# A decoder layer on one core: two queues for the first loads, x turned inside a job, another sharing of the last scaling

## The chip, the cores and the metric

The kernel runs on one core of one Trainium2 chip. The metric is the device time of one execution in microseconds (us), the median of several runs. The core's engines are called TensorE (PE, matmuls; PEld, its weight loads), VectorE (DVE), ScalarE (ACT), GpSimd (POOL) and SyncE (SP), which here only issues DMAs. ScalarE and GpSimd can issue DMAs too; each issuing engine has a queue of its own.

## The reference

One layer on 256 tokens of width 2048, in float32:

```python
h = rmsnorm(x, ln1)
dq, dk, dv, sq, sk, sv = split(h @ w_in)          # w_in: 2048 x 6144
mixed = concat([rmsnorm(diff_attention(rotary(dq), rotary(dk), dv, lam), diff_head_norm),
                rmsnorm(stick_breaking_attention(sq, sk, sv), sb_head_norm)])
x = x + mixed @ w_out                              # 2048 x 2048
h = rmsnorm(x, ln2)
x = x + square(relu(h @ w_mlp_in)) @ w_mlp_out     # 2048 x 8192, 8192 x 2048
out = rmsnorm(x, ln_f)
```

The two attentions have eight heads each; lam comes from four small vectors of 64. The sizes of the four weight matrices, some 200 MB together, set the work.

## The kernel before

The tokens are two tiles of 128 (t = 0, 1). Each weight matrix is read in chunks of 4 k-tiles (128 rows each) by 512 columns, 1 MB a chunk; a chunk makes two jobs of two k-tiles. For a job, `issue_conv` (L201) splits its weights into a high part `wh` (a cast on ScalarE, L214) and a low part `wl` (the difference, on VectorE, L217); the activations are held as such a pair too, and `products_acc` (L250) makes three matmuls per k-tile and token tile: high by high, high by low, low by high. A job is thus 12 matmuls of 512 columns (L260 to L262).

x lies with tokens on partitions. `x_pair` (L311) turns two k-tiles of it with four transposes on TensorE (L319) and scales them by ln1: ScalarE writes the high half (L149), VectorE the low half (L151). The scales, `g1T`, are made in the first `x_pair`: a small transpose of `rows1` and a copy on VectorE (L286). `keep_clock_up` (L291) issues matmuls on zeros that nothing reads.

Between a start and the rest the order of the work is set in two ways. In the start, TensorE, ScalarE and VectorE get their instructions in the order in which the program calls them: `START_ORDER` (L39) names the steps, x for `x_pair`, c for `issue_conv`, m for a job's matmuls. So the low half of the first weights stands behind the first x pair on VectorE. SP, GpSimd and all that comes after the start are ordered by a planner.

The loads are issued by `issue_dma` (L177), all from SP: for chunk 0 half of the columns of x's first tile, `rows1` (ln1), the first half of the chunk, the other half of x's columns, the second half of the chunk; for the next chunks one tile of x and the chunk. `small_loads` (L85), eight DMAs for ln2, the head norms, the rotary table and the four lambda vectors, follows chunk 3.

At the end, `second_token_tile` (L754) makes the last 512 columns of token tile 1 in two halves of 256 columns; `finish_tokens` (L790) then computes the scale `rf` of each token and scales the four blocks of 512 columns (nb = 0 to 3). Blocks 0 to 2 have been multiplied by ln_f before; block 3 is multiplied by `rf` and ln_f in one three-operand pass (L817). Block 1 is ScalarE's, the others VectorE's, in five pieces; each piece is written out by a DMA from SP, block 1's from ScalarE (L822).

Of the kernel before, what the change touches and what calls it, by code (L numbers as in the profile page):

```python
# [14 lines left out]
ALU = mybir.AluOpType  # L15
# [3 lines left out]
P = 128  # L19
S = 256  # L20
# [3 lines left out]
KT = D // P  # L24
NB = 512
CK = 4
HK = 2
# [8 lines left out]
LAM_INIT = 0.8 - 0.6 * math.exp(-0.3 * 0)  # L36
W_BUFS = 3
S_BUFS = 4
START_ORDER = "x0 c0 x1 c1 m0 x2 c2 m1 c3 x3 m2 x4 c4 m3 c5 x5 m4 x6 c6 m5 c7 x7 m6"  # L39
WARM0, WARM1 = 5, 4  # L40
AHEAD = 3


# [1 line left out]
def tile_hybrid_layer(  # L45
# [19 lines left out]


    nc = tc.nc
    nc.scalar.preload_act_table_set("natural_log_exp_and_others")

    cpool = ctx.enter_context(tc.tile_pool(name="cpool", bufs=1))  # L70
    wpool = ctx.enter_context(tc.tile_pool(name="wpool", bufs=W_BUFS))
    spool = ctx.enter_context(tc.tile_pool(name="spool", bufs=S_BUFS))
# [4 lines left out]
    x_v = x[0].rearrange("(t p) c -> p t c", p=P)  # L77
    xt = [cpool.tile([P, NT, NB], F32, tag=f"x{nb}", name=f"x{nb}") for nb in range(4)]

    rows1 = cpool.tile([KT, P], F32, name="rows1")  # L80
    rows2 = cpool.tile([KT + 2, P], F32, name="rows2")
    lamv = cpool.tile([P, 4, 64], F32, name="lamv")
    rope_t = cpool.tile([P, NT, 2, 16], F32, name="rope_t")

    def small_loads():  # L85
        nc.sync.dma_start(rows2[0:KT, :], ln2[0].rearrange("(k p) -> k p", p=P))
        nc.sync.dma_start(rows2[KT:KT + 1, :], diff_head_norm)
        nc.sync.dma_start(rows2[KT + 1:KT + 2, :], sb_head_norm)
        nc.sync.dma_start(rope_t, rope)
        for i, l in enumerate((lambda_q1, lambda_k1, lambda_q2, lambda_k2)):  # L90
            nc.sync.dma_start(lamv[:, i, :], l[0].partition_broadcast(P))


    idle = cpool.tile([P, NB], BF16, name="idle")
# [68 lines left out]
    chunks = []  # L163
# [11 lines left out]
    state = {"dma": 0, "conv": 0, "job": 0, "ahead": AHEAD}  # L175

    def issue_dma():  # L177
        c = state["dma"]
        if c < len(chunks):
            pool = mlp["w"] if "w" in mlp and c % 2 else wpool  # L180
            t = pool.tile([P, CK, NB], F32, tag="w", name=f"w{c}")
            if c == 0:
                for h in range(2):
                    cs = slice(h * S, (h + 1) * S)
                    nc.sync.dma_start(xt[0][:, :, cs], x_v[:, :, cs])
                    if h == 0:
                        nc.sync.dma_start(rows1, ln1[0].rearrange("(k p) -> k p", p=P))
                    nc.sync.dma_start(t[:, h * HK:(h + 1) * HK, :], chunks[0][:, h * HK:(h + 1) * HK, :])
            else:
                if c < len(xt):  # L190
                    nc.sync.dma_start(xt[c], x_v[:, :, c * NB:(c + 1) * NB])
                step = HK if c == 1 else CK
                for k in range(0, CK, step):
                    ks = slice(k, k + step)
                    nc.sync.dma_start(t[:, ks, :], chunks[c][:, ks, :])
            if c == 3:
                small_loads()
            wt[c] = t
            state["dma"] += 1
# [50 lines left out]
    def products_acc(get_acc, act, k0, first, last):  # L250
        def f(h, wh, wl):
            acc = get_acc()
            for j in range(HK):
                kt = k0 + h * HK + j
                a = act(kt)
                for t in range(NT):
                    st = slice(t * P, (t + 1) * P)
                    s0 = first and h == 0 and j == 0
                    s1 = last and h == CK // HK - 1 and j == HK - 1
                    nc.tensor.matmul(acc[t], a[:, 0, st], wh[:, j, :], start=s0, stop=False)  # L260
                    nc.tensor.matmul(acc[t], a[:, 0, st], wl[:, j, :], start=False, stop=False)  # L261
                    state["mm"] = nc.tensor.matmul(acc[t], a[:, 1, st], wh[:, j, :], start=False, stop=s1)  # L262
        return f

    xs = [None] * (KT // HK)
# [25 lines left out]
    def keep_clock_up(n, name):  # L291


        warm = ps_acc.tile([P, NB], F32, tag="acc", name=f"warm_{name}")
        for _ in range(n):
            nc.tensor.matmul(warm, idle[:, :P], idle, start=True, stop=True)
# [14 lines left out]
    def x_pair(p2):  # L311
        if p2 == 0:
            gT[1] = norm_columns(rows1, KT, "g1T")
        pool, tag = ((ps_tp, "tp"), (ps_o, "o"))[p2 % 2]
        tp = pool.tile([P, HK * S], F32, tag=tag, name=f"xtp{p2}")
        for j in range(HK):
            kt = p2 * HK + j
            for t in range(NT):
                nc.tensor.transpose(tp[:, j * S + t * P:j * S + (t + 1) * P],  # L319
                                    xt[kt // 4][:, t, (kt % 4) * P:(kt % 4 + 1) * P], ident)  # L320
        if p2 == 0:
            keep_clock_up(WARM1, "b")
        xs[p2] = apool.tile([P, HK, 2, S], F32R, tag="act", name=f"xs{p2}")
        split_pair(xs[p2], tp, gT[1][:, p2 * HK:(p2 + 1) * HK], True)

# [370 lines left out]
    def out_group(q, nb):  # L696
# [33 lines left out]
        half = NB // 2  # L730
# [23 lines left out]
        def second_token_tile(hc):  # L754
            def f(h, wh, wl):
                o = acc[1] if hc == 0 else bank("ma_last")
                cs = slice(hc * half, (hc + 1) * half)
                for kt in range(KT):
                    passes(o[:, :half], 1, cs, kt, kept[kt // HK])
                residual(nb, 1, o[:, :half], cs)  # L760
                if hc == 1:
                    base = square_base(1, nb + 1)
                square_sum(nb, 1, cs, nb + hc)
                if hc == 1:
                    finish_tokens(1, base)
            return f
# [12 lines left out]
    def square_sum(nb, t, cs, i):  # L779
        y = xt[nb][:, t, cs]  # L780
        junk = cpool.tile([P, NB], F32, tag="junk", name=f"junk3{nb}{t}{i}")
        nc.scalar.activation(junk[:, cs], y, AF.Square, accum_out=ss3[:, t, i:i + 1])
# [7 lines left out]
    def finish_tokens(t, base):  # L790

        last = ss3[:, t, 3 + t:4 + t]
        vm = tiny.tile([P, 1], F32, tag="fvm", name=f"fvm{t}")
        nc.vector.tensor_scalar(vm, last, base, BIG, op0=ALU.add, op1=ALU.min)
        lv = tiny.tile([P, 1], F32, tag="flv", name=f"flv{t}")
        nc.scalar.activation(lv, vm, AF.Ln, bias=eps_c, scale=LN_IN / D)
        r0 = tiny.tile([P, 1], F32, tag="fr0", name=f"fr0{t}")
        nc.scalar.activation(r0, lv, AF.Exp, scale=-0.5, bias=lnout_c)
        v = tiny.tile([P, 1], F32, tag="fv", name=f"fv{t}")
        nc.vector.tensor_scalar(v, vm, 1.0 / D, EPS, op0=ALU.mult, op1=ALU.add)  # L800
        ok = tiny.tile([P, 1], F32, tag="fok", name=f"fok{t}")
        nc.vector.tensor_scalar(ok, last, base, FMAX, op0=ALU.add, op1=ALU.is_le)
        nc.vector.tensor_scalar_mul(ok, ok, -0.5)
        a = tiny.tile([P, 1], F32, tag="fa", name=f"fa{t}")
        nc.vector.tensor_tensor(a, v, r0, op=ALU.mult)
        nc.vector.scalar_tensor_tensor(a, a, r0, three_c, op0=ALU.mult, op1=ALU.subtract)
        rf = cpool.tile([P, 1], F32, tag=f"rf{t}", name=f"rf{t}")
        nc.vector.scalar_tensor_tensor(rf, a, r0, ok, op0=ALU.mult, op1=ALU.mult)
        o_v = out[0, t * P:(t + 1) * P, :]
        h = NB // 2  # L810
        pieces = [(nc.vector, 0, 0, h), (nc.scalar, 1, 0, NB), (nc.vector, 0, h, NB), (nc.vector, 2, 0, NB),
                  (nc.vector, 3, 0, NB)]
        for eng, nb, c0, c1 in pieces:
            y = xt[nb][:, t, c0:c1]
            cs = slice(nb * NB + c0, nb * NB + c1)
            if nb == 3:
                nc.vector.scalar_tensor_tensor(y, y, rf, lnf_t[:, cs], op0=ALU.mult, op1=ALU.mult)  # L817
            elif eng is nc.scalar:
                nc.scalar.activation(y, y, AF.Copy, scale=rf)
            else:  # L820
                nc.vector.tensor_scalar_mul(y, y, rf)
            (nc.scalar if eng is nc.scalar else nc.sync).dma_start(o_v[:, cs], y)  # L822

    for q in range(FQ):
        for g in range(FG):
# [6 lines left out]
        issue_dma()  # L832
    with tc.manual_schedule(engines={mybir.EngineType.PE, mybir.EngineType.Activation, mybir.EngineType.DVE}):
        state["ahead"] = 0
        keep_clock_up(WARM0, "a")
        for step in START_ORDER.split():
            {"x": x_pair, "c": lambda i: issue_conv(), "m": lambda i: run_jobs(i + 1)}[step[0]](int(step[1]))
    state["ahead"] = AHEAD
    run_jobs(n_out0)
    while any(m is None for m in mixT):  # L840
# [4 lines left out]
    lnf_t = mlp["sb"].tile([P, D], F32, tag="lnf", name="lnf_t", bufs=1)  # L845
# [57 lines left out]
```

## Time and profile before

| | us |
|---|---|
| runs: median of 3 (lowest, highest) | 1110.95 (1110.37, 1111.13) |
| profiled execution, its own time | 1109.93 |
| span of the profile | 1108.2 |
| TensorE busy | 1095.4 (99%) |
| VectorE busy | 647.8 (58%) |
| ScalarE busy | 519.4 (47%) |
| GpSimd busy | 121.0 (11%) |
| DMA: 222.35 MB at a mean of 201 GB/s | |

The span reaches from the first to the last instruction of the core; the execution's own time is 1.7 us more. Times in the views count from the span's start. Matmuls overlap in their pipeline, so that one lasts longer (0.39 us) than the distance to the next. A row of the timeline merges equal neighbours: its length is then that of the whole run of them.

### The profile page before, as it was taken

The numbers are of one execution on the slowest core, as the hardware profiler recorded it, in microseconds if no ns is written. First come the engines' busy times: TensorE is split into PE (matmuls) and PEld (weight loads), VectorE is DVE, ScalarE is ACT, GpSimd is POOL, SyncE is SP. The second block draws the span as 40 slices with busy tenths as digits, with TensorE's granted clock in tenths as the row PEclk, the third lists the DMA queues.
The fourth block names the chain that finished last, engine by engine and source line by source line (L and its number), as shares of the span: only waits on it lengthen the run. The fifth ranks groups of instructions, "written<-read, shape, count | busy, mean of one in ns | idle before, by whom it ended". The sixth has DMA issues, their size and how long they took to land.

```text
span 1108.2 us, 13750 instructions
## 1 busy us (share of the span) xinstructions
PE 1095.4 (99%) x5019; PEld 905.7 (82%) x5019; DVE 647.8 (58%) x798; ACT 519.4 (47%) x665; POOL 121.0 (11%) x240
## 2 busy tenths in 40 slices
PE   8999999999999999999999999999999999999996
PEld 6887888888887888888888888888888888888886
DVE  5756766656456665565554665545566544655752
ACT  5655555555555554444333444333444333444541
POOL 1111101101100212230001111000211000131000
PEclk9999999999999999999999999999999999999999
DMA  8675555646646885765666765656676566667512
GB/s 293 203 252 168 184 181 162 197 155 188 208 153 230 312 257 176 260 224 197 198 193 195 240 215 191 210 190 194 188 248 215 196 197 198 214 192 247 191 38 77
DMA packets 130296, 222.35 MB, mean 201 GB/s; under 512 B 11282, under 2 KB 26676, under 8 KB 130100
## 3 DMA queue, kind: packets, MB, share of 16 engines
q1 hardware_dynamic: 122772, 213.59, 58.3%
q0 software_dynamic: 7168, 7.35, 2.6%
q8 instruction: 39, 0.64, 0.2%
q10 hardware_dynamic: 288, 0.52, 0.1%
q14 instruction: 29, 0.24, 0.1%
HBM read 204.65 MB, written 2.10 MB: 187 GB/s over the span
## 4 chain that ended last, share of the span: by engine, by line
PE 98%; DMA 0%; DVE 0%; ACT 0%; SPq 0%; issue 0%; DVEq 0%; ACTq 0%
PE ia L260 10%; PE ia L262 10%; PE ia L261 10%; PE ma L261 10%; PE ma L262 10%; PE ma L260 10%; PE oacc L260 3%; PE oacc L262 3%; PE oacc L261 3%; PE acc_dk L260 1%; PE acc_dq L261 1%; PE acc_sk L260 1%; PE acc_sq L260 1%; PE acc_dq L262 1%; PE acc_sk L261 1%; PE acc_dq L260 1%
## 5 line engine op out<-in xcount | busy, mean ns | idle before, releaser
L217 DVE TENSOR_TENSOR wl<-w,wh 128x1024 fp32r<-128x1024 f32 (+1 forms) x385 | 468.7, 1221 | 393.7 <-ACT wh L214 392.7
L214 ACT CAST wh<-w 128x1024 fp32r<-128x1024 f32 (+1 forms) x385 | 402.2, 1049 | 501.8 <-PE ia L262 196.8
L261 PE MATMUL ia<-wl,xs 128*128 128x512 f32 x512 | 199.0, 389 | 0.0
L262 PE MATMUL ia<-wh,xs 128*128 128x512 f32 x512 | 198.6, 389 | 0.0
L260 PE MATMUL ia<-wh,xs 128*128 128x512 f32 x512 | 198.5, 389 | 0.0
L260 PE MATMUL ma<-wh,aT 128*128 128x512 f32 x480 | 186.3, 389 | 0.0
L261 PE MATMUL ma<-wl,aT 128*128 128x512 f32 x480 | 186.3, 389 | 0.0
L262 PE MATMUL ma<-wh,aT 128*128 128x512 f32 x480 | 185.5, 389 | 0.0
L378 POOL DMA_DIRECT2D hT<-bl x128 | 67.4, 535 | 529.9 <-DMA w<-in_w_mlp_in_dram 244.3
L262 PEld LDWEIGHTS ia<-wh,xs 128*128 128x128 f32 x512 | 96.1, 188 | 20.0
L261 PEld LDWEIGHTS ia<-wl,xs 128*128 128x128 f32 x512 | 96.1, 188 | 19.9
L260 PEld LDWEIGHTS ia<-wh,xs 128*128 128x128 f32 x512 | 96.1, 188 | 19.9
L260 PEld LDWEIGHTS ma<-wh,aT 128*128 128x128 f32 x480 | 90.1, 188 | 18.7
L261 PEld LDWEIGHTS ma<-wl,aT 128*128 128x128 f32 x480 | 90.1, 188 | 18.7
L262 PEld LDWEIGHTS ma<-wh,aT 128*128 128x128 f32 x480 | 90.1, 188 | 18.7
L260 PE MATMUL oacc<-wh,mixT 128*128 128x512 f32 x128 | 49.9, 391 | 1.3 <-ACT mixT L156 1.3
L261 PE MATMUL oacc<-wl,mixT 128*128 128x512 f32 x128 | 50.1, 392 | 0.0
L262 PE MATMUL oacc<-wh,mixT 128*128 128x512 f32 x128 | 49.4, 389 | 0.0
L378 POOL DMA_DIRECT2D x2T<-x2bl x32 | 16.8, 534 | 114.6 <-DVE x L615 72.7
L260 PEld LDWEIGHTS oacc<-wh,mixT 128*128 128x128 f32 x128 | 24.0, 188 | 6.3 <-ACT mixT L156 1.5
L261 PEld LDWEIGHTS oacc<-wl,mixT 128*128 128x128 f32 x128 | 24.1, 188 | 4.9
L262 PEld LDWEIGHTS oacc<-wh,mixT 128*128 128x128 f32 x128 | 24.0, 188 | 4.8
(227 smaller groups left out, 1219.9 us busy)
## 6 DMA issues: line engine op xcount, KB each, us to landing
w<-in_w_mlp_in_dram SPq DMA_DIRECT2D x64, 1024.0 KB, 5.4
w<-in_w_mlp_out_dram SPq DMA_DIRECT2D x64, 1024.0 KB, 5.1
w<-in_w_in_dram SPq DMA_DIRECT2D x46, 1024.0 KB, 5.1
w<-in_w_out_dram SPq DMA_DIRECT2D x16, 1024.0 KB, 5.4
hT<-bl SPq DMA_DIRECT2D x128, 32.0 KB, 1.9
hT<-bl POOLq DMA_DIRECT2D x128, 32.0 KB, 1.8
w<-in_w_in_dram SPq DMA_DIRECT2D x4, 512.0 KB, 7.7
x<-in_x_dram SPq DMA_DIRECT2D x3, 512.0 KB, 10.1
```

The lines of the kernel that those rows point to most:

```text
L214: state["wh"] = nc.scalar.copy(wh[:, j], w[:, j])
L217: state["wl"] = nc.vector.tensor_tensor(wl[:, j], w[:, j], wh[:, j].bitcast(F32), op=ALU.subtract)
L260: nc.tensor.matmul(acc[t], a[:, 0, st], wh[:, j, :], start=s0, stop=False)
L261: nc.tensor.matmul(acc[t], a[:, 0, st], wl[:, j, :], start=False, stop=False)
L262: state["mm"] = nc.tensor.matmul(acc[t], a[:, 1, st], wh[:, j, :], start=False, stop=s1)
L378: engines[(i * 4 + f) % len(engines)].dma_start(dv[f * 32:(f + 1) * 32, :, i, :], bl[i * 32:(i + 1) * 32, :, f, :])
```

## The change

The loads of x's first tile and of ln1 move from SP to ScalarE's queue, ahead of ScalarE's table load. SP loads chunk 0 in three pieces (one k-tile, one k-tile, two k-tiles). The small loads move from SP to GpSimd. The written-out order of the start becomes: six matmuls on zeros (before five, and four more after the first transposes), the first conversion, the first x pair; then for each job the next conversion and the job, in which the next x pair is turned after the job's first six matmuls. At the end, the first half of block 3 of token tile 1 is multiplied by ln_f as soon as it is there. The pieces come in another order: block 3 first, then blocks 1, 2, 0; block 1 and half of block 0 are ScalarE's, and these two are written out by GpSimd, the others by SP. Block 3 is written out as a whole.

```diff
-START_ORDER = "x0 c0 x1 c1 m0 x2 c2 m1 c3 x3 m2 x4 c4 m3 c5 x5 m4 x6 c6 m5 c7 x7 m6"
-WARM0, WARM1 = 5, 4
+WARM = 6
...
-    nc.scalar.preload_act_table_set("natural_log_exp_and_others")
...
     rows1 = cpool.tile([KT, P], F32, name="rows1")
+    nc.scalar.dma_start(xt[0][:, :, 0:S], x_v[:, :, 0:S])
+    nc.scalar.dma_start(rows1, ln1[0].rearrange("(k p) -> k p", p=P))
+    nc.scalar.dma_start(xt[0][:, :, S:NB], x_v[:, :, S:NB])
+    nc.scalar.preload_act_table_set("natural_log_exp_and_others")
...
     def small_loads():
-        nc.sync.dma_start(rows2[0:KT, :], ln2[0].rearrange("(k p) -> k p", p=P))
+        nc.gpsimd.dma_start(rows2[0:KT, :], ln2[0].rearrange("(k p) -> k p", p=P))
...
             if c == 0:
-                for h in range(2):
-                    cs = slice(h * S, (h + 1) * S)
-                    nc.sync.dma_start(xt[0][:, :, cs], x_v[:, :, cs])
-                    if h == 0:
-                        nc.sync.dma_start(rows1, ln1[0].rearrange("(k p) -> k p", p=P))
-                    nc.sync.dma_start(t[:, h * HK:(h + 1) * HK, :], chunks[0][:, h * HK:(h + 1) * HK, :])
+                for ks in (slice(0, 1), slice(1, 2), slice(2, 4)):
+                    nc.sync.dma_start(t[:, ks, :], chunks[0][:, ks, :])
...
                     state["mm"] = nc.tensor.matmul(acc[t], a[:, 1, st], wh[:, j, :], start=False, stop=s1)
+                if j == 0 and "mid" in state:
+                    x_pair(state.pop("mid"))
...
-        if p2 == 0:
-            keep_clock_up(WARM1, "b")
...
                 square_sum(nb, 1, cs, nb + hc)
+                if hc == 0:
+                    nc.vector.tensor_tensor(xt[nb][:, 1, cs], xt[nb][:, 1, cs],
+                                            lnf_t[:, nb * NB:nb * NB + half], op=ALU.mult)
...
-        pieces = [(nc.vector, 0, 0, h), (nc.scalar, 1, 0, NB), (nc.vector, 0, h, NB), (nc.vector, 2, 0, NB),
-                  (nc.vector, 3, 0, NB)]
-        for eng, nb, c0, c1 in pieces:
+        if t == 0:
+            last3 = [(3, 0, NB, nc.vector, True, nc.sync)]
+        else:
+            last3 = [(3, h, NB, nc.vector, True, None), (3, 0, h, nc.vector, False, nc.sync)]
+        for nb, c0, c1, eng, lnf, queue in last3 + [
+                (1, 0, NB, nc.scalar, False, nc.gpsimd), (2, 0, NB, nc.vector, False, nc.sync),
+                (0, 0, h, nc.scalar, False, nc.gpsimd), (0, h, NB, nc.vector, False, nc.sync)]:
...
-            (nc.scalar if eng is nc.scalar else nc.sync).dma_start(o_v[:, cs], y)
+            if queue is not None:
+                if nb == 3:
+                    c1 = NB
+                queue.dma_start(o_v[:, nb * NB + c0:nb * NB + c1], xt[nb][:, t, c0:c1])
...
-        keep_clock_up(WARM0, "a")
-        for step in START_ORDER.split():
-            {"x": x_pair, "c": lambda i: issue_conv(), "m": lambda i: run_jobs(i + 1)}[step[0]](int(step[1]))
+        keep_clock_up(WARM, "a")
+        issue_conv()
+        x_pair(0)
+        for i in range(KT // HK - 1):
+            issue_conv()
+            state["mid"] = i + 1
+            run_jobs(i + 1)
```

## Rows read from the trace of the kernel before

**Rows 1.** The page, its first part: engine, busy us, share of the span, instructions.

```profile
PE 1095.4 (99%) x5019; PEld 905.7 (82%) x5019; DVE 647.8 (58%) x798; ACT 519.4 (47%) x665; POOL 121.0 (11%) x240
```

**Rows 2.** TensorE's waits: line, what it waited for, total us, times, longest.

```profile
PE oacc L260 <- ACT mixT L156: 1.3, 1, 1.3
```

**Rows 3.** The chain of waits at the start: start us, us, what.

```profile
2.28 4.92 DMA x<-in_x_dram
7.24 0.66 PE xtp L319 x4
```

**Rows 4.** Stretches of the end: busy us per engine, granted clock, DMA share, GB/s.

```profile
1099.54:1102.28 2.74, 0.00 (x1) 0.00 (x0) 1.61 (x8) 1.10 (x4) 0.00 (x0) 1.00 0.00 0
1103.50:1106.50 3.00, 0.00 (x0) 0.00 (x0) 0.48 (x1) 0.00 (x0) 0.00 (x0) 0.58 0.97 350
```

**Rows 5.** Groups by shape, first 25 us: busy us, mean ns | idle before.

```profile
L214 ACT CAST wh<-w 128x512 fp32r<-128x512 f32 x2 | 1.1, 616 | 0.5 <-DMA w<-in_w_in_dram 0.5
L217 DVE TENSOR_TENSOR wl<-w,wh 128x512 fp32r<-128x512 f32 x2 | 1.3, 688 | 0.3 <-ACT wh L214 0.3
L286 DVE COPY g1T<-ps_g1T 128x16 f32<-128x16 f32 x1 | 0.2, 175 | 1.6 <-PE ps_g1T L284 1.6
L149 ACT ACTIVATE xs<-xtp,g1T 128x256 fp32r<-128x256 f32 x14 | 5.9, 471 | 10.5 <-PE xtp L319 10.5
```

**Rows 6.** Timeline at the start: start us, us, engine, line, operation, tiles.

```profile
0.81 0.44 SPq L185 DMA_DIRECT2D x<-in_x_dram  x1
0.81 1.28 ACT L68 ACT_TABLE_LOAD   x1 [0.81 <-PEq L888]
1.26 2.31 PE L296 MATMUL warm_a<-idle 128*128 128x512 bf16 x5 [1.26 <-DVE three_c L105]
4.16 0.99 PE L319 MATMUL xtp<-ident,x 128*128 128x128 f32 x4
4.98 1.03 PE L296 MATMUL warm_b<-idle 128*128 128x512 bf16 x4
6.55 1.14 ACT L214 CAST wh<-w 128x512 fp32r<-128x512 f32 x2 [0.53 <-DMA w<-in_w_in_dram]
```

**Rows 7.** The DMA issued at 0.81: KB, us from issue to landing.

```profile
x<-in_x_dram SPq DMA_DIRECT2D x1, 256.0 KB, 2.9
```

**Rows 8.** Stretches of the start, columns as in group 4.

```profile
1.90:3.60 1.70, 1.67 (x4) 0.30 (x2) 0.29 (x1) 0.19 (x1) 1.68 (x7) 1.00 0.77 198
3.60:7.24 3.64, 2.04 (x9) 1.28 (x9) 1.09 (x4) 1.53 (x4) 0.00 (x0) 1.00 0.92 295
7.24:10.50 3.26, 3.26 (x16) 2.71 (x17) 2.88 (x5) 2.23 (x4) 0.00 (x0) 1.00 1.03 366
```

**Rows 9.** Groups of GpSimd, columns as in group 5.

```profile
L378 POOL DMA_DIRECT2D hT<-bl x128 | 67.4, 535 | 529.9 <-DMA w<-in_w_mlp_in_dram 244.3 <-ACT wh L214 123.5 <-DMA hT<-bl 104.3
```

**Rows 10.** The timeline at the end.

```profile
1102.31 1.01 DVE L821 TENSOR_SCALAR x<-x,rf 128x256 f32<-128x256 f32 x3
1102.69 1.85 SPq L822 DMA_DIRECT2D out_dram<-x  x4
```

**Rows 11.** Groups by shape, 1088 to 1108.2 us.

```profile
L817 DVE SCALAR_TENSOR_TENSOR x<-x,rf,lnf_t 128x512 f32<-128x512 f32 x2 | 1.5, 746 | 0.0
L821 DVE TENSOR_SCALAR x<-x,rf 128x256 f32<-128x256 f32 x4 | 1.2, 351 | 0.1
L821 DVE TENSOR_SCALAR x<-x,rf 128x512 f32<-128x512 f32 x2 | 1.0, 482 | 0.0
L819 ACT ACTIVATE x<-x,rf 128x512 f32<-128x512 f32 x2 | 1.5, 726 | 1.5 <-DVE rf L808 1.5
```

**Rows 12.** DMA queues, 1104.4 to 1104.85 us: packets, MB, share; ScalarE's last issue.

```profile
q10 hardware_dynamic: 54, 0.09, 55.7%
q1 hardware_dynamic: 64, 0.07, 42.0%
out_dram<-x ACTq DMA_DIRECT2D x1, 256.0 KB, 2.3
```

More of the change, by code (lines that the diff above doesn't have):

```diff
@@ L85, in small_loads @@
     def small_loads():
-        nc.sync.dma_start(rows2[0:KT, :], ln2[0].rearrange("(k p) -> k p", p=P))
-        nc.sync.dma_start(rows2[KT:KT + 1, :], diff_head_norm)
-        nc.sync.dma_start(rows2[KT + 1:KT + 2, :], sb_head_norm)
-        nc.sync.dma_start(rope_t, rope)
+        nc.gpsimd.dma_start(rows2[0:KT, :], ln2[0].rearrange("(k p) -> k p", p=P))
+        nc.gpsimd.dma_start(rows2[KT:KT + 1, :], diff_head_norm)
+        nc.gpsimd.dma_start(rows2[KT + 1:KT + 2, :], sb_head_norm)
+        nc.gpsimd.dma_start(rope_t, rope)
         for i, l in enumerate((lambda_q1, lambda_k1, lambda_q2, lambda_k2)):
-            nc.sync.dma_start(lamv[:, i, :], l[0].partition_broadcast(P))
+            nc.gpsimd.dma_start(lamv[:, i, :], l[0].partition_broadcast(P))
     idle = cpool.tile([P, NB], BF16, name="idle")
@@ L810, in finish_tokens @@
         h = NB // 2
-        pieces = [(nc.vector, 0, 0, h), (nc.scalar, 1, 0, NB), (nc.vector, 0, h, NB), (nc.vector, 2, 0, NB),
-                  (nc.vector, 3, 0, NB)]
-        for eng, nb, c0, c1 in pieces:
+        if t == 0:
[5 more added lines that the diff above has]
+                (0, 0, h, nc.scalar, False, nc.gpsimd), (0, h, NB, nc.vector, False, nc.sync)]:
             y = xt[nb][:, t, c0:c1]
             cs = slice(nb * NB + c0, nb * NB + c1)
-            if nb == 3:
+            if lnf:
                 nc.vector.scalar_tensor_tensor(y, y, rf, lnf_t[:, cs], op0=ALU.mult, op1=ALU.mult)
```

## Prediction

> **What bounds the kernel now.** I read four views, in this order. First the page's busy times: TensorE is busy 1095.4 of 1108.2 us [rows 1], so no edit to another engine matters unless it moves TensorE's first or last instruction or opens a hole between. Second, TensorE's waits: between start and end the one hole is 1.3 us at the output projection [rows 2], which no edit touches. Third, the chain at the start: it runs through the second half of x's first tile, which comes after 4.92 us in the queue; TensorE begins its unbroken stream with the four transposes of it at 7.24 us [rows 3]. Fourth, the stretches of the end: TensorE stops at 1099.54, the last norm takes until 1102.28, and from 1103.5 to about 1106.5 the DMA engines move the last token tile's 1 MB at a share of 0.97 and 350 GB/s [rows 4]. The span ends 1.7 us later. So only two stretches are in play: 7.24 us ahead of the stream and 8.66 us behind it. In the second the final 3.0 us is a transfer at full share, not an engine.
>
> **The change at the start.** The stream's first matmul needs four things: the high half of the first weight slice, its low half, the x columns turned, and those scaled by g1T. The order in which the engines are given work is written out, so each works strictly in it. Before, x's turning came ahead of weight conversion; after, both conversions (two pieces of 512 columns each on ScalarE, then on VectorE) stand ahead of VectorE's g1T copy and of ScalarE's scaling of x. Behind VectorE's wait for the second piece of weights there are now queued g1T's copy and, behind it, the low halves of x.
>
> So the gate is T, the landing of the second 256 KB piece of weights. From T on, one after the other, with hops of about 0.03 us: cast 0.62, difference 0.69, g1T copy 0.18, scaling 0.47 [rows 5]. With the hops that is 2.1 us, and the first matmul starts at S = T + 2.1.
>
> T itself: x's first half, the scales and the two weight pieces are 795 kB. Both queues begin at 0.81, where SP begins now [rows 6]. Lower end: the second piece is issued one issue later, at about 1.3, and takes the 2.9 us that a 256 KB load took alone [rows 7]: T = 4.2. Upper end: now the same 795 kB (x half, scales, 512 KB of weights) are ahead of the cast that could start at 6.55 [rows 6]; T is no later than that, 6.5, as everything is issued earlier. Between: from 1.90 on, when data starts, 795 kB at the 295 GB/s of the stretch that follows [rows 8] end at 4.6; the lone load landed about 0.5 us after its 262 kB had passed at 198 GB/s (1.90 + 1.32 = 3.22 against 0.81 + 2.9 = 3.71) [rows 7, 8], so 5.1. I take T = 5.2, nearest to that row; S = 7.3, with ends 6.3 and 8.6.
>
> The stream's work is the same as before, since it includes the transposes of x's second half either way (they now stand after six matmuls of the first job). The stream starts at 7.3 instead of 7.24: **+0.06 us, from -0.9 to +1.4.** That the earlier weights gain nothing is because the conversion and the copy, which lay beside the wait for x, now stand on the path.
>
> The other edits here I cost at nothing, with this cover. The transfer of x's first half now shares the engines with weights (5.2 rather than 3.7), but its transposes, 0.99 us [rows 6], and g1T's are done before T + 1.4, when VectorE comes to the copy. ScalarE's three issues, at SP's 0.44 us each, and the 1.28 us table load behind them [rows 6] end near 3.4, ahead of its first use. Moved into the middle of a job, the turning of x leaves ScalarE and VectorE half a job less to scale it; in the stretch of a first job and what follows it, 3.26 us, they are busy 2.23 and 2.88 us [rows 8], so VectorE has 0.4 us to spare, and if that is used up the cost is a few tenths once. The eight small loads leave SP, whose later weight loads stand behind them, and go to GpSimd, whose issue takes 0.54 us [rows 9]: 4.3 us behind its masks, nothing waits for it there. Their few hundred small packets run beside weights that have some 0.7 us to spare; without this cover, at most 0.5 us.
>
> **The change at the end.** Count from R = 1102.28, when the scale is known. Before: the first piece was 256 columns, 0.35 us, so SP's first issue came at 1102.69, R + 0.41 [rows 10], and data at R + 1.22 [rows 4]. After: VectorE first does 256 columns of the last block by the three-operand form, for which 512 columns take 0.75 [rows 11]; half of that with its fixed part is 0.45. Then 256 plain columns, 0.35; SP's first issue is at R + 0.81. GpSimd's first follows ScalarE's 0.73 [rows 11] at R + 0.78. Nothing is issued earlier, so data starts at R + 0.81 + 0.81 = R + 1.62, 0.4 us later than now. The rest follows in time to keep 16 engines fed: SP's other issues are ready at R + 1.2 and R + 1.6, GpSimd's second at R + 1.3. The bytes are the same, in rows of the same lengths, and where two queues had data together they moved packet for packet (54 beside 64) [rows 12], so the 3.0 us stay 3.0 us. VectorE ends 0.2 us earlier, but this is not what the end waits for: **+0.4 us.** Ends: the transfer can be shorter if GpSimd's queue feeds it better; 1.05 MB at the 366 GB/s of the fastest stretch read [rows 8] are 2.9 us, and half of the later start may be made up if its pieces come closer, so +0.1; GpSimd's issues of 256 KB may take twice its 0.54 us, which puts its last data 0.5 us after the others: +0.9. The new product of 256 columns by ln_f for the second token tile, and all of the first tile's pieces, lie beside matmuls that run until 1099.54: nothing.
>
> A three-operand pass of 512 columns takes 0.75 us, a plain one 0.48 and 256 plain ones 0.35 [rows 11]: the plain form goes through 256 more columns in 0.13 us, the faster of two rates. For such passes the Trainium skill (SBUF — State Buffer, section "SBUF: two separate sides") says that VectorE then holds a port that GpSimd needs to write a DMA's descriptors, so that GpSimd's DMA waits until the pass ends. Whether it does here no row shows. By the rows alone the end is +0.4; by the rule GpSimd's first piece waits until VectorE is through, and that is the third rival.
>
> **Sum.** +0.06 + 0.4 = about +0.45 us. The profiled execution has 1109.93 us, a span of 1108.2 and 1.7 around it; it is 1.0 us below the median of the runs, 1110.95. Against its own time: 1110.4; against the median: **1111.4 us.** A change below 0.2% (2.2 us) can't be told from none in this kernel, so this is "the same".
>
> **Rivals.**
> 1. *The loads win.* T is 4.2: both queues together ramp up as fast as one did alone. For it: the stretch 1.9 to 3.6 moved 198 GB/s against 366 later [rows 8], so there is room early. Against: the shared packets. S = 6.3, -0.9; with the end between +0.1 and +0.4 the time is about 1110.3.
> 2. *The clock stays low; slower.* The first five warming matmuls stand 0.43 us apart (2.31 for five, 512 columns each: 1.2 GHz); four of the same take 1.03 after 4.98 (2.4 GHz) [rows 6]. So the rise came at about 4.9, after 3.6 us of nearly unbroken work. The four that carried it on are taken out, and x's first half comes later: TensorE is idle from about 3.9 (six at 0.43 from 1.26) to about 5, does transposes, and is idle again until S. If the clock is low at S, the stream runs at half rate until it rises: 3.6 to 4.9 us at half rate lose 1.8 to 2.4, say 2.1: 1113.5. Against: the sixth warming matmul makes the first stretch longer, and at the end the granted clock fell late: its mean of 0.58 over 1103.5 to 1106.5 [rows 4] is 1.0 for 0.5 us and then 0.5, so it fell at about 1104, over 4 us after the last matmul, and a gap of 2 us need not lower it. It decides as soon as the first matmuls stand 0.45 us apart.
> 3. *GpSimd is held up at the end.* Its first issue waits from R + 0.78 to R + 1.45, when VectorE is through; with doubled issue time the second ends at R + 3.6, and its 128 KB land some 2 us on (ScalarE's 256 KB took 2.3 [rows 12]), at R + 5.6. In the forecast the data ends at R + 4.6 and lands 0.5 later, so this is 0.45 more: 1111.8. Against: GpSimd's first piece needn't be there before the others have run out, at about R + 3.5.
> 4. *ScalarE loads its table ahead of its DMAs*, so the change doesn't start two queues at once. x's first half is then issued at 2.1 and lands near 5.9, with its transposes done at 7.1 and S = 7.7: +0.4, 1111.8.
>
> **How the numbers follow.** Chances: forecast 0.50 (own range 1110.4 to 1112.3), first rival 0.22, second 0.13, third 0.08, fourth 0.04; 0.03 for what I don't see. Range 1109.6 to 1113.3: it takes in both ends of the start, most of the first rival and half of the second. Faster by over 0.2% (under 1108.7) is more than both lower ends give (-0.8), so it needs something that I don't see, as the 1.3 us hole gone too [rows 2]: 0.06. Slower by over 0.2% (over 1113.2) is most of the second rival and a rest: 0.13. Within: 0.81.
>
> **What would show it.** The cast of the second weight piece starts at T; g1T's copy follows VectorE's second difference, and the first matmul is 2.1 us after T. If the copy runs earlier, the step on order is wrong. The first matmuls stand 0.23 us apart, or 0.45 if the second rival holds. At the end, data starts 1.6 us after the scale, and the stretch of full share is still 3 us. I am wrong outright if TensorE's stream starts before 6.3 or after 8.6, or if holes open in it after the first two jobs.

## The result, and the profile after

The changed kernel takes 1119.01 us, the median of 5 runs (1118.66 to 1119.82); the kernel before took 1110.95 us in the same session (1110.37 to 1111.18). The ratio is 1.0077, interval 1.0066 to 1.0089: slower by 8.1 us, outside my range of 1109.6 to 1113.3. The profiled execution has 1118.66 us and a span of 1117.0, against 1109.93 and 1108.2 before. TensorE's work is nearly unchanged, and the 1.3 us hole in the middle is still there. This is the page's first part, and TensorE's waits (columns as in [rows 2]):

```profile
PE 1096.9 (98%) x5016; PEld 907.1 (81%) x5016; DVE 647.8 (58%) x798; ACT 520.5 (47%) x667; POOL 127.8 (11%) x252
```

```profile
PE ps_g1T L283 <- DMA rows<-in_ln_dram: 1.8, 1, 1.8
PE oacc L257 <- ACT mixT L157: 1.3, 1, 1.3
PE acc_dq L257 <- ACT xs L150: 0.6, 1, 0.6
```

So the loss lies at the two ends. TensorE's last matmul ends at 1101.85 in place of 1099.54, and the span ends 15.1 us behind it in place of 8.7: 2.3 us at the start, 6.5 at the end.

**The end.** The stretches after the last norm (R, when the scale is known, is now about 1104.6; columns as in [rows 4]):

```profile
1104.60:1106.50 1.90, 0.00 (x0) 0.00 (x0) 1.41 (x4) 1.12 (x2) 0.88 (x2) 0.50 0.15 57
1106.50:1109.00 2.50, 0.00 (x0) 0.00 (x0) 0.00 (x0) 0.00 (x0) 0.19 (x1) 0.50 0.96 343
1109.00:1111.00 2.00, 0.00 (x0) 0.00 (x0) 0.00 (x0) 0.00 (x0) 0.00 (x0) 0.50 0.13 41
1111.00:1117.00 6.00, 0.00 (x0) 0.00 (x0) 0.00 (x0) 0.00 (x0) 0.00 (x0) 0.50 0.00 0
```

The transfer has the size and share it had in [rows 4]. Then come 6 us in which nothing computes and nothing moves. The answer is in the instructions that stand for no line of the program's work. They are attributed to its last line, here L910. This view of that line gives the operation, its count, the shortest, median and longest duration in ns, and the first and last start:

```profile
L910 SPq EVENT_SEMAPHORE  x12: 17/28/2849, 1106.7 to 1116.9; - x12
L910 POOLq EVENT_SEMAPHORE  x4: 17/17/17, 1116.2 to 1116.8; - x4
L910 POOLq DRAIN  x3: 46/107/10030, 1106.1 to 1116.7; - x3
L910 SPq DRAIN  x3: 7/7/7, 1110.2 to 1116.4; - x3
```

GpSimd's queue closes with a DRAIN of 10.03 us. It starts at 1106.1, as its last store is issued, and ends at 1116.2. SyncE has seen everything land by 1110.2 and then waits for GpSimd. The chain of waits (start us, us, what) runs through GpSimd's stores too, and its last row is GpSimd's queue at this same line:

```profile
1095.45 0.56 POOL out_dram L830
1096.01 9.60 issue
1105.61 0.04 POOLq L830
1105.65 0.51 POOL out_dram L830
1106.16 0.53 POOLq L910
```

The drain is not the stores' own transfer. GpSimd's two stores land 3.1 and 3.6 us after their issue (the issues of 1105 to 1110 us: KB, us to landing), so by 1109.8:

```profile
out_dram<-x SPq DMA_DIRECT2D x2, 256.0 KB, 2.9
out_dram<-x POOLq DMA_DIRECT2D x1, 256.0 KB, 3.1
out_dram<-x POOLq DMA_DIRECT2D x1, 128.0 KB, 3.6
```

The kernel before has the same drain. It starts where GpSimd's work ended, 91 us ahead of the span's end, and was covered. The same view of its last line:

```profile
L898 POOLq DRAIN  x3: 34/102/9207, 1016.9 to 1107.9; - x3
```

**The start.** The timeline of the first 12 us (columns as in [rows 6]):

```profile
1.26 2.74 PE L295 MATMUL warm_a<-idle 128*128 128x512 bf16 x6 [1.26 <-DVE three_c L106]
5.57 0.62 ACT L211 CAST wh<-w 128x512 fp32r<-128x512 f32 x1 [0.68 <-DMA w<-in_w_in_dram]
5.84 0.25 PE L283 MATMUL ps_g1T<-ident,rows 16*128 16x16 f32 x1 [1.83 <-DMA rows<-in_ln_dram]
6.02 1.11 PE L318 MATMUL xtp<-ident,x 128*128 128x128 f32 x4
6.82 0.17 DVE L285 COPY g1T<-ps_g1T 128x16 f32<-128x16 f32 x1
7.17 0.84 ACT L150 ACTIVATE xs<-xtp,g1T 128x256 fp32r<-128x256 f32 x2 [0.99 <-PE xtp L318]
7.70 0.80 PE L257 MATMUL acc_dq<-wh,xs 128*128 128x512 f32 x1 [0.56 <-ACT xs L150]
9.18 0.63 PE L257 MATMUL acc_dq<-wh,xs 128*128 128x512 f32 x1
9.61 0.63 PE L258 MATMUL acc_dq<-wl,xs 128*128 128x512 f32 x1
12.04 0.39 PE L259 MATMUL acc_dq<-wh,xs 128*128 128x512 f32 x1
12.26 0.39 PE L257 MATMUL acc_dq<-wh,xs 128*128 128x512 f32 x1
```

The stream starts at 7.70, within 0.04 us of before. But its first matmuls stand 0.43 us apart, 512 columns at 1.2 GHz, until about 11.7; from 12.04 on they stand 0.22 apart, 2.4 GHz. (The clock column of the stretches below reads 1.00 here, where this profile has no record of the clock yet; the spacing is the evidence.) At the same time the weights slow down. The stretches, of the changed kernel and then of the one before:

```profile
7.70:9.80 2.10, 2.10 (x5) 1.53 (x6) 1.70 (x3) 1.25 (x2) 0.64 (x2) 1.00 1.08 350
9.80:11.90 2.10, 2.10 (x9) 1.71 (x8) 0.41 (x1) 0.35 (x1) 0.00 (x0) 1.00 1.19 138
11.90:14.00 2.10, 2.10 (x11) 1.73 (x10) 0.88 (x2) 1.18 (x3) 0.00 (x0) 1.00 0.90 266
```

```profile
7.70:9.80 2.10, 2.10 (x11) 1.69 (x10) 1.72 (x5) 1.78 (x3) 0.00 (x0) 1.00 1.03 358
9.80:11.90 2.10, 2.10 (x13) 1.77 (x12) 1.18 (x1) 0.70 (x2) 0.00 (x0) 1.00 1.04 399
11.90:14.00 2.10, 2.10 (x12) 1.72 (x11) 1.87 (x3) 2.02 (x3) 0.00 (x0) 1.00 1.06 410
```

From 9.80 to 11.90 the DMA engines are no less busy than before (1.19 against 1.04), but move 138 GB/s in place of 399. By queue (packets, MB, share of 16 engines), GpSimd's queue q0, with the small loads, takes most of the time for a sixth of the bytes:

```profile
q0 software_dynamic: 44, 0.05, 77.8%
q1 hardware_dynamic: 122, 0.24, 40.9%
```

That leaves two theories for the 2.3 us at the start, the low clock and the late weights, and one for the end, GpSimd's drain.

### The profile page after: what moved, and what is told of

It is laid out like the page before. It is cut to its first block, busy times and chain, and to the rows that moved or that the text cites. A ratio compares the mean times of both kernels' runs of the same rounds, so it can differ in the third digit from the quotient of the medians.

```text
span 1117.0 us, 13755 instructions
## 1 busy us (share of the span) xinstructions
PE 1096.9 (98%) x5016; PEld 907.1 (81%) x5016; DVE 647.8 (58%) x798; ACT 520.5 (47%) x667; POOL 127.8 (11%) x252
## 4 chain that ended last, share of the span: by engine, by line
PE 90%; issue 8%; POOL 0%; DMA 0%; ACT 0%; POOLq 0%; ACTq 0%
PE ia L259 10%; PE ia L258 10%; PE ia L257 10%; PE ma L259 8%; PE ma L257 8%; PE ma L258 8%; PE oacc L257 3%; PE oacc L258 3%; PE oacc L259 3%; PE acc_dq L257 1%; PE acc_dq L259 1%; PE acc_dq L258 1%; PE acc_dk L257 1%; PE acc_sk L257 1%; PE acc_sq L257 1%
```

## The experiments

The kernel before was run beside each: 1110.76 us in the session of the first two runs on the end and the first two on the start, 1110.57 in that of the last of the four kernels and of the candidate, 1110.75 in that of the others.

### The end

**All last pieces off GpSimd.** The changed kernel, with the four pieces on ScalarE's queue:

```diff
-                (1, 0, NB, nc.scalar, False, nc.gpsimd), (2, 0, NB, nc.vector, False, nc.sync),
-                (0, 0, h, nc.scalar, False, nc.gpsimd), (0, h, NB, nc.vector, False, nc.sync)]:
+                (1, 0, NB, nc.scalar, False, nc.scalar), (2, 0, NB, nc.vector, False, nc.sync),
+                (0, 0, h, nc.scalar, False, nc.scalar), (0, h, NB, nc.vector, False, nc.sync)]:
```

> The changed kernel, with the last pieces that GpSimd wrote out issued by ScalarE instead; all else as changed. Theory: at the program's end GpSimd drains for 10.0 us after its last DMA (its row in the changed kernel), and that is waited for; with no DMA of its late in the program the drain lies under the matmuls, and SyncE's last wait (1110.2, then 0.8 of closing) ends the span at about 1111.0 instead of 1117.0: about 6 us less, 1113.0. Rival: the end is longer because the data starts later and comes by another queue; the data's end moved by 0.5 us only, so this queue gives back at most that: 1118.5.

Measured: 1113.10 us (10 runs), ratio to the kernel before 1.0021 (1.0012 to 1.003). The 5.9 us are gone. The drain is still there, now at 1018.6, under the matmuls:

```profile
L910 POOLq DRAIN  x3: 46/102/10085, 1018.6 to 1110.4; - x3
```

**One store on GpSimd, alone.** The kernel before, with block 1 of token tile 1 stored by GpSimd:

```diff
-            (nc.scalar if eng is nc.scalar else nc.sync).dma_start(o_v[:, cs], y)
+            q = nc.sync if eng is not nc.scalar else nc.gpsimd if t == 1 else nc.scalar
+            q.dma_start(o_v[:, cs], y)
```

> The kernel before, with one thing changed: the one piece of the second token tile that ScalarE wrote out (256 KB) is issued by GpSimd. Theory of the drain: GpSimd issues at about 1103.1, takes 0.5, and its drain (9.2 us in the kernel before, where it ended at 1026) ends at about 1112.8; with 0.8 of closing the span is 1113.6 instead of 1108.2, so about 1116.3. Rival, that only data and landing count: between 0 and 0.6 us more, 1111.5 at most.

Measured: 1115.49 us (4 runs), ratio 1.0046 (1.0031 to 1.0061). One 256 KB store costs 4.7 us because it moves the drain to 1103.9:

```profile
L899 POOLq DRAIN  x3: 46/102/9175, 1103.9 to 1113.6; - x3
```

**GpSimd for the first token tile only.**

```diff
-  (1, 0, NB, nc.scalar, False, nc.gpsimd), ... (0, 0, h, nc.scalar, False, nc.gpsimd)
+  (1, 0, NB, nc.scalar, False, nc.gpsimd if t == 0 else nc.scalar), ...  # and the same for block 0
```

> The changed kernel with GpSimd issuing the two scaled pieces of token tile 0 only; those of token tile 1 go to ScalarE's queue. Theory (the closing drain of GpSimd takes some 10 us from its last DMA, and costs only what of it lies behind the end of the other engines): tile 0's last piece is issued near 1096, the drain is over by about 1106, before the last landings; time as with all four pieces on ScalarE's queue, 1113.1 us (1112.4 to 1113.7). Rival (a store issued by GpSimd costs its price wherever it stands, for example by slower writes): 1115 or more.

Measured: 1113.10 us (10 runs), the same as with no store on GpSimd. The drain runs from 1095.5 for 9.9 us, beside the last matmuls, and costs nothing. So it is the place of GpSimd's last DMA that counts, not the store. The drain:

```profile
L910 POOLq DRAIN  x3: 46/108/9895, 1095.5 to 1110.9; - x3
```

**Fewer DMAs on GpSimd.** The kernel with one store on GpSimd, and its share of the hT turns (128 DMAs) moved to SyncE:

```diff
-            turn(hT, bl, [acc[t] for t in range(NT)], [nc.sync, nc.gpsimd])
+            turn(hT, bl, [acc[t] for t in range(NT)], [nc.sync])
```

> The kernel before with block 1 of token tile 1 stored by GpSimd (as in the run that gave 1115.5), and with the 128 transfers of the hT turns that GpSimd issued moved to SyncE, so that GpSimd issues 65 DMAs in all and not 193. If the closing drain's length goes with the number of DMAs that GpSimd issued: 9.2 x 65/193 = 3.1 us, over before the other engines end, so 1111 us (up to 1112, if SyncE's queue pays for the turns). If its length is fixed: 1115.5 us as before.

Measured: 1115.91 us (4 runs). With 128 DMAs fewer the drain is 8.60 us. My counts were off: by the traces GpSimd issues 97 DMAs here and 225 in the kernel with one store, so that in proportion the drain would be 4.0 us, not 3.1; it is neither. Its length hardly depends on how much GpSimd has issued:

```profile
L899 POOLq DRAIN  x3: 46/102/8602, 1104.4 to 1113.5; - x3
```

Nor is it a backlog of earlier DMAs: ahead of its one store GpSimd had been idle for 683 us (columns as in [rows 6]):

```profile
1104.40 0.58 POOL L823 DMA_DIRECT2D out_dram<-x  x1 [682.93 <-ACT x L819]
```

### The start

**More warming alone.** The changed kernel, with 12 warming matmuls and 4 more behind the first transposes:

```diff
-WARM = 6
+WARM, WARM1 = 12, 4
...
+        if p2 == 0:
+            keep_clock_up(WARM1, "b")
```

> The changed kernel, with twelve instead of six warming matmuls ahead of the first transposes and four behind those of the first x pair, so that TensorE is not idle between 4.0 and 5.8 us and less between 7.1 and 7.7. Theory of the clock: the first job's matmuls go at 0.23 us instead of 0.43 apart, as the clock is up when the stream begins; 4.2 us at half rate become 2.1, so about 2 us less: 1117.0. Rival, that the start is late for its loads and the order on VectorE: the stream begins where it did, and nothing is gained (1119.0), or the added matmuls delay it (1119.5).

Measured: 1118.72 us (4 runs), against 1119.01. The first job ran at the higher clock, and then TensorE stalled at weights that were not there: at 15.62 and 22.63 its next matmul came 0.6 and 0.3 us late, the first of these a wait for the low half (columns as in [rows 2]). My expectation of 1117.0 failed: something else holds the same jobs back.

```profile
PE acc_dq L258 <- DVE wl L214: 0.4, 1, 0.4
```

**Warming, and the last pieces on ScalarE's queue** (both diffs above):

> Both edits in the changed kernel: the last pieces from ScalarE's queue and the added warming matmuls. If the drain and the clock are all of the loss, 6 and 2 us are given back: 1111.0, equal to the kernel before within 0.5 us, with what is left in the later data at the end (0.4) and the first matmul (0.4). If a third thing is behind it, the time stays over 1112.

Measured: 1112.43 us (10 runs), above 1112, which I had named as the sign of a third thing. From 6 to 34 us ScalarE waits 5.4 us for weights (columns as in [rows 2]; the profile is that of the slowest of these runs, 1113.29 us):

```profile
ACT wh L211 <- DMA w<-in_w_in_dram: 5.4, 5, 3.1
```

**The small loads back on SyncE,** added to the last kernel:

```diff
     def small_loads():
-        nc.gpsimd.dma_start(rows2[0:KT, :], ln2[0].rearrange("(k p) -> k p", p=P))
+        nc.sync.dma_start(rows2[0:KT, :], ln2[0].rearrange("(k p) -> k p", p=P))
...
```

> The changed kernel with the last pieces on ScalarE's queue and the longer warming (the run that gave 1112.4), and with the small loads back on SyncE's queue. Theory (the small loads on GpSimd's queue slow the weights of the first jobs): the first eight jobs fall from 25.2 to about 22.5 us and the time to what is left, +0.3 us at the start and +0.4 us at the end over the kernel before, so 1111.6 us at most, 1110.4 to 1112.0. Rival (the pieces and the second queue slow the weights, wherever the small loads go): 1112.4 us, eight jobs in 25 us.

Measured: 1111.08 us (11 runs), ratio 1.0003 (0.9995 to 1.0012). ScalarE's wait for weights in the same stretch falls to 0.9 us, and from 9.80 to 11.90 the DMA engines move 408 GB/s, where the kernel with the loads on GpSimd moves 148. That kernel's stretch, this kernel's, and this kernel's wait:

```profile
9.80:11.90 2.10, 2.10 (x13) 1.76 (x12) 1.74 (x3) 0.84 (x2) 0.00 (x0) 1.00 1.14 148
```

```profile
9.80:11.90 2.10, 2.10 (x13) 1.79 (x12) 1.45 (x3) 1.53 (x3) 0.00 (x0) 1.00 1.06 408
```

```profile
ACT wh L211 <- DMA w<-in_w_in_dram: 0.9, 2, 0.7
```

The eight jobs took 23.3 us in its profile, not the 22.5 expected. Part of this is that x's second turn now stands inside the stream; in the kernel before it stood ahead of it.

**The small loads on SyncE, but the change's 6 warming matmuls,** which makes four kernels that differ in two things:

> The changed kernel with the last pieces on ScalarE's queue and the small loads back on SyncE's, but with the change's 6 warming matmuls (the clock's cause alone; with 16 warming matmuls the same gave 1111.1 us). Theory (a low clock in the first job and late weights each cost about 2 us and hide each other, since both hold back the same three jobs): the clock is low until 10.8 to 11.9 us, the first eight jobs take 24 to 24.5 us, time 1112.6 to 1113.2 us. Rival (the prices add up; the clock is worth 0.7 us, the difference that the warming made beside the late weights): 1111.8 us.

Measured: 1113.14 us (11 runs), ratio 1.002 (1.0012 to 1.0029): the theory's number, not the rival's 1111.8. The weights are on time (407 GB/s from 9.80 to 11.90), but the matmuls still start 0.43 us apart until 13.3, and the eight jobs take 25.3 us. Both are more than expected (10.8 to 11.9, and 24 to 24.5); the profile is that of one of the two slowest runs, 1113.48 us. The runs spread from 1112.06 to 1113.49, where those with 12 and 4 warming matmuls lie between 1110.98 and 1111.36, so what the low clock costs seems to vary by the execution, from 1 to 2.4 us. One matmul ahead of the rise and one behind it:

```profile
12.46 0.63 PE L259 MATMUL acc_dq<-wh,xs 128*128 128x512 f32 x1
13.58 0.39 PE L259 MATMUL acc_dq<-wh,xs 128*128 128x512 f32 x1
```

The four, all with the last pieces on ScalarE's queue (medians, us):

```
                         6 warming    12 + 4 warming
small loads on GpSimd     1113.10        1112.43
small loads on SyncE      1113.14        1111.08
```

Together the two cost 2.02 us. Either alone costs 2.06 (clock) or 1.35 (weights). The four are from three sessions; against the kernel before of each session these are 2.01, 2.24 and 1.34. They don't add up: while the clock is low, TensorE uses the weights slowly, and late ones cost nothing that can be told (1113.10 against 1113.14; the changed kernel's TensorE, in its waits above, never waits for weights). Mending one of them gives back at most 0.7 us.

**The small loads alone, in the kernel before:**

> The kernel before with one part of the change alone: the eight small loads on GpSimd's queue. Theory (they slow the weight chunks that are under way beside them): the third job's weights come 1 to 1.5 us later, the first eight jobs take 24 to 25 us in place of 22.5, the time is 1112.5 to 1113.5 us. Rival (the weights have slack for it, the lateness came from the order of pieces): 1111.0 us, eight jobs in 22.5 us.

Measured: 1112.22 us (11 runs from 1111.57 to 1115.13, ratio 1.0016, 1.0007 to 1.0025), 1.5 us more than the kernel before and somewhat under the expected 1112.5. In its profile the DMA engines move 189 GB/s from 9.80 to 11.90. But the clock stayed low there until 12.4 too, so this run doesn't part the two causes; why the clock was late is open.

### A candidate

The kernel before with its own end, one weight piece and the rows on ScalarE's queue, and x turned in the middle of a job:

```diff
-WARM0, WARM1 = 5, 4
+WARM0, WARM1 = 6, 6
...
+                nc.scalar.dma_start(rows1, ln1[0].rearrange("(k p) -> k p", p=P))
+                nc.scalar.dma_start(t[:, 0:1, :], chunks[0][:, 0:1, :])
+                nc.scalar.preload_act_table_set("natural_log_exp_and_others")
+                nc.sync.dma_start(xt[0][:, :, 0:S], x_v[:, :, 0:S])
+                nc.sync.dma_start(t[:, 1:2, :], chunks[0][:, 1:2, :])
+                nc.sync.dma_start(xt[0][:, :, S:NB], x_v[:, :, S:NB])
+                nc.sync.dma_start(t[:, 2:4, :], chunks[0][:, 2:4, :])
...
+        x_pair(0)
+        issue_conv()
+        for i in range(KT // HK - 1):
+            issue_conv()
+            state["mid"] = i + 1
+            run_jobs(i + 1)
```

> A candidate: the kernel before with its own end and its small loads on SyncE's queue; at the start only ln1's rows and the first 256 KB weight piece go to ScalarE's queue, x's two halves and the other pieces stay on SyncE's, x is turned ahead of the first cast and the next pair in the middle of a job, and there are 6 and 6 warming matmuls. If the start is set by the landings (x first half 4.9 us, weight piece about 5.3): ScalarE scales x until 6.0 and casts until 6.7, first matmul of acc_dq near 6.9 in place of 7.66, time 1110.0 us (1109.7 to 1110.5). Rival (more pieces share one bandwidth, so that x lands later by what the weights land earlier; or the third job then waits for its weights): first matmul 7.5 or later, or the gain lost by the eighth job, 1110.7 to 1111.3 us.

Measured: 1110.06 us (11 runs) against 1110.57, ratio 0.9996 (0.9987 to 1.0005): no difference that can be told. The first matmul does come at 6.99, 0.67 us earlier, but the second waits for the low half of the weights, and TensorE reaches acc_dk, the work behind the eight jobs, at 30.34, where the kernel before did at 30.18. So the time is in the theory's range, but the path is the rival's, the gain lost by the eighth job; the number is no sign for the theory. The first two matmuls:

```profile
6.99 0.50 PE L259 MATMUL acc_dq<-wh,xs 128*128 128x512 f32 x1 [0.95 <-ACT wh L213]
7.72 0.50 PE L260 MATMUL acc_dq<-wl,xs 128*128 128x512 f32 x1 [0.23 <-DVE wl L216]
```

## Why the prediction was wrong

Of the 8.06 us, 5.91 are GpSimd's closing drain (1119.01 less 1113.10), 2.02 the start (1113.10 less 1111.08), and 0.13 are left. Against the kernel before of each session they are 5.72, 2.01 and 0.33; what is left can't be told from nothing, nor from the +0.45 that I forecast.

**The step that failed: "GpSimd's second at R + 1.3 ... the 3.0 us stay 3.0 us ... +0.4 us".** I took the end to be the last landing and costed GpSimd by its issues and by a port, never by what its queue does after its last DMA. Its closing drain would have started at R + 1.3 and ended at R + 10.5 by the 9.2 us that stood in the trace of before. The landings I forecast ended at about R + 5. That was 5 to 6 us to be seen beforehand, and neither a rival nor my end of +0.9 held it. None of the signs that I named as being wrong outright came either: they all watched TensorE's stream. Without the drain the time, 1113.10, stands inside my range, but by the second rival's clock, not by the forecast's path. A row that costs nothing where it stands is a price as soon as the work ahead of it moves.

**The data at the end: right.** With R about 1104.6, SyncE's first store came at 1105.38, R + 0.8 as forecast, the data near R + 1.6, and the stretch at full share took about 3 us. In the four kernels of the table, with the drain covered, the end behind the last matmul is that of the data alone: 9.0 to 9.1 us in their profiles (span less the end of the last matmul), against 8.7 before. This is the +0.4.

**T and S: right within their ranges.** T was forecast at 5.2 (4.2 to 6.5) and was 5.5, where the second cast starts. S = T + 2.1 = 7.6; the first matmul came at 7.70, which is +0.46 on the 7.24 of the prediction and not +0.06. But the path was not quite mine: g1T's copy did follow VectorE's second difference (ending at 6.99), and ScalarE's scaling then waited for TensorE's transposes, which ended at 7.13. They had waited until 5.84 for ln1's rows and ran at the lower clock. It was nearly a tie.

**The clock: the second rival, which I gave 0.13, is what happened.** It priced 2.1 us and the pair on SyncE measures 2.06 (medians). In the changed kernel TensorE was idle for the rows from 4.0 to 5.84, after 2.74 us of warming, and the four transposes then took 1.11 us, where the second group of before took 0.66 [rows 3]: the clock was not up. My reason against the rival was that a gap of about 2 us need not lower a clock once risen. The run with all last pieces on ScalarE's queue, whose start is the same program, speaks against that reason. There the transposes took 0.65 us after the same gap, so the clock had risen, and the stream, which began 1.0 us behind them, still went 0.42 us apart (the granted clock is 0.50 from 7.70 to 9.80):

```profile
6.00 0.65 PE L318 MATMUL xtp<-ident,x 128*128 128x128 f32 x4
8.21 0.63 PE L258 MATMUL acc_dq<-wl,xs 128*128 128x512 f32 x1
8.63 0.66 PE L259 MATMUL acc_dq<-wh,xs 128*128 128x512 f32 x1
```

So the same start meets the clock differently in two executions; what decides it is open.

**The small loads: mis-sized.** "At most 0.5 us" without the cover; they cost 1.35 with the clock up. I counted issue slots and bytes, not the DMA time that their packets take on that queue. With the clock low they cost nothing that can be told, so the time of the changed kernel alone would not have shown this.

**The first rival** is out, T was 5.5. So is **the fourth**: the table load comes at 2.28, behind ScalarE's three DMAs; that its S of 7.7 was met is luck. **The third** foresaw the right engine for a wrong reason. By the Trainium skill (SBUF — State Buffer, section "SBUF: two separate sides"), VectorE's fast passes keep GpSimd from writing descriptors. Here GpSimd's two issues took 0.54 us each, as elsewhere [rows 9], the first beginning at R + 1.0, 0.3 us behind ScalarE's piece as for token tile 0, while VectorE was still at work; it landed after 3.1 us, SyncE's of the same size after 2.9. So this trace shows no such delay.

## What to carry to other kernels

Before a DMA is moved to another engine's queue, look at what that queue does behind its last one: an instruction that now lies under other work becomes the end of the kernel when the work ahead of it moves there. Two causes that hold back the same jobs hide each other, so that mending one shows little; four kernels, with each on and off, give the prices. Small loads are not free because they are small: price them by the DMA time of their queue.

## What was not expected of the hardware

GpSimd's queue closed with a drain of 8.6 to 10.1 us in every profile of this study. It was 9.2 us in the kernel before, where GpSimd issues 224 DMAs, and 8.6 where it issues 97, so mostly fixed. With the eight small loads on GpSimd it was 9.9 to 10.1. In the changed kernel it went on 6.4 us after the last landing. What it waits for is open. In every kernel here GpSimd's last work is a DMA, so whether a queue that has issued none closes this way is not shown.

Small loads on GpSimd's queue took 77.8% of the DMA engines' time for 0.05 MB in 2.1 us. The Trainium skill (DMA: Bandwidth & Descriptors, section "Issuing engines are not separate DMA queues") says that DMAs of all issuing engines share the same 16 DMA engines, and that several issuers save only issue time. The shared engines agree with these rows. That the issuer otherwise doesn't matter they do not bear out: the same eight loads left 148 GB/s when issued by GpSimd, and 408 when issued by SyncE in its own order behind the first chunks. But more than the queue differs. As the profiles record packets, GpSimd's queue moved the eight loads in the changed kernel from 6.5 to 15.9 us, beside the weights, in 256 of them; 80 of them, of 2 KB, took 0.55 us each. In the kernel before SyncE's queue moved nearly all the same bytes as 640 packets of 256 bytes, 0.017 us each, from 16.7 us on, behind the first chunks. The queue, the form of the packets and the place in time change together, and no run here parts them.
